# Splitting the first load of a split-GELU-multiply kernel by partitions

## The chip, the cores and the metric

The kernel runs on one core of a Trainium2 chip. The metric is the device time of one execution in microseconds. Times given are medians of several executions; besides them there is one execution taken by the hardware profiler, with its own span.

A core has compute engines that run side by side, each with its own queue of instructions. Three matter here: ScalarE (ACT in the profile), VectorE (DVE) and SyncE (SP), which only issues transfers. Transfers are carried out by 16 DMA engines, which belong to the core and serve all its queues. On-chip memory is an array of 128 partitions; a tile lies across them.

## The reference

The input `x` is 32 x 512 x 2048 float32. Its last axis is cut in two halves; the first goes through the exact GELU and is multiplied with the second:

```python
half_dim = x.shape[-1] // 2
x1, x2 = (x[..., :half_dim].copy(), x[..., half_dim:].copy())
gelu_x1 = 0.5 * x1 * (1 + erf(x1 / np.sqrt(2)))
return (gelu_x1 * x2).astype(np.float32)
```

So 134.22 MB are read and 67.11 MB written, with two operations for each element of the output.

## The kernel before

The 16,384 rows of 2048 numbers are cut into 16 tiles of 1024 rows. In a tile each of the 128 partitions holds R = 8 consecutive rows, which lie side by side in DRAM, 64 KB in one piece. There are two buffers for `x` tiles (8 MB each) and two for output tiles (4 MB each); tile i uses buffer i % 2. Tensors and semaphores are placed by hand, and the order on each engine is the order of the calls.

`load` (its transfer is issued at L47) puts a load on SP's queue. `store` (issued at L54) puts a store on a queue given to it, behind a wait for all multiplies so far. Every transfer adds 16 to a semaphore when it has landed. The page calls the queue of SP q1 and that of ACT q10.

Three loads are issued ahead of everything: rows 0 to 3 of every partition of tile 0 (32 KB in each, 4 MB in all; semaphore `first[0]`), rows 4 to 7 of tile 0 (`first[1]`), and the whole of tile 1 (`ready[1]`). Then `tc.close()` (L67) puts a barrier over the engines.

The loop over tiles comes next. In the first and the last tile the work is cut into steps of 2, 2 and 4 rows, in the others into 5 and 3 rows. In each step ACT applies GELU from the `x` tile's first half into the output tile (L81), and DVE multiplies the output tile by the `x` tile's second half in place (L89). ACT waits for the load ahead of a tile's first step; in tile 0 it waits for `first[0]` ahead of the first step and for `first[1]` ahead of the third. After a tile's last multiply SP issues the load of tile i + 2 into the same buffer. Stores are issued from ACT's queue, those of the last two tiles from SP's. A tile's load and the store of the tile two before it share a semaphore, so that ACT's one wait covers both.

At the end the semaphores are cleared (ACT at L114, DVE at L116, SP at L117), and SP waits at L118 for the last three stores.

Of the kernel before, what the change touches and what calls it, by code (L numbers as in the profile page):

```python
# [1 line left out]

# [4 lines left out]

GELU = mybir.ActivationFunctionType.Gelu


@with_exitstack
def kernel(
    ctx: ExitStack,
    tc: tile.TileContext,
    x: bass.AP,
    out: bass.AP,
):
    nc = tc.nc
    P = nc.NUM_PARTITIONS

    x_flat = x.flatten_outer_dims()
    out_flat = out.flatten_outer_dims()
    n_rows, dim = x_flat.shape
    half = dim // 2

    R = 8
    x_t = x_flat.rearrange("(n p r) d -> n p r d", p=P, r=R)
    o_t = out_flat.rearrange("(n p r) d -> n p r d", p=P, r=R)
    n_tiles = x_t.shape[0]
    x_bufs = [nc.alloc_sbuf_tensor(f"x{k}_tile", [P, R, dim], x.dtype) for k in range(2)]  # L30
    o_bufs = [nc.alloc_sbuf_tensor(f"o{k}_tile", [P, R, half], out.dtype) for k in range(2)]

    first = [nc.alloc_semaphore(f"first{j}") for j in range(2)]
    ready = [nc.alloc_semaphore(f"ready{k}") for k in range(2)]
    gelu_done = nc.alloc_semaphore("gelu_done")
    mul_done = nc.alloc_semaphore("mul_done")
    tail_stored = nc.alloc_semaphore("tail_stored")
    n = {sem.name: 0 for sem in [*first, *ready, gelu_done, mul_done, tail_stored]}  # L40

    def counted(ins, sem, by):
        ins.then_inc(sem, by)
        n[sem.name] += by

    def load(i, rows, sem):
        ins = nc.sync.dma_start(out=x_bufs[i % 2][:, rows, :], in_=x_t[i][:, rows, :])  # L47
        counted(ins, sem, 16)
        return ins

    def store(queue, i, rows, sem):
        queue.wait_ge(mul_done, n[mul_done.name])
        counted(
            queue.dma_start(out=o_t[i][:, rows, :], in_=o_bufs[i % 2][:, rows, :]), sem, 16  # L54
        )

    for ins in (  # L60
        load(0, slice(0, 4), first[0]),
        load(0, slice(4, 8), first[1]),
        load(1, slice(0, 8), ready[1]),
    ):
        tc.no_tile_sem_insts.add(ins.ins.name)
    tc.close()
    tc.compile()  # L67

    for i in range(n_tiles):
        k = i % 2  # L70
        last = i == n_tiles - 1
        pieces = i == 0 or last
        steps = ((0, 2), (2, 4), (4, 8)) if pieces else ((0, 5), (5, 8))
        for lo, hi in steps:
            rows = slice(lo, hi)
            if i == 0 and lo % 4 == 0:
                nc.scalar.wait_ge(first[lo // 4], 16)
            elif lo == 0:
                nc.scalar.wait_ge(ready[k], n[ready[k].name])
            counted(  # L80
                nc.scalar.activation(  # L81
                    out=o_bufs[k][:, rows, :], in_=x_bufs[k][:, rows, :half], func=GELU
                ),
                gelu_done,
                1,
            )
            nc.vector.wait_ge(gelu_done, n[gelu_done.name])
            counted(
                nc.vector.tensor_mul(  # L89
                    out=o_bufs[k][:, rows, :],  # L90
                    in0=o_bufs[k][:, rows, :],
                    in1=x_bufs[k][:, rows, half:],
                ),
                mul_done,
                1,
            )
            if pieces and hi % 4 == 0:
                if last:
                    store(nc.sync, i, slice(hi - 4, hi), tail_stored)
                else:  # L100
                    store(nc.scalar, i, slice(hi - 4, hi), ready[k])
        if not pieces:
            if i == n_tiles - 2:
                store(nc.sync, i, slice(0, R), tail_stored)
            else:
                store(nc.scalar, i, slice(0, R), ready[k])
        if i + 2 < n_tiles:
            nc.sync.wait_ge(mul_done, n[mul_done.name])
            load(i + 2, slice(0, R), ready[k])


    nc.scalar.drain()  # L112
    for sem in (*first, *ready):
        nc.scalar.sem_clear(sem)  # L114
    nc.vector.drain()
    nc.vector.sem_clear(gelu_done)  # L116
    nc.sync.sem_clear(mul_done)  # L117
    nc.sync.wait_ge(tail_stored, n[tail_stored.name]).then_inc(  # L118
        tail_stored, -n[tail_stored.name]
    )  # L120


# [1 line left out]
_INS = ['x']  # L124
_OUTS = [((32, 512, 1024), 'float32')]


# [23 lines left out]
```

## Time and profile before

| what | us |
|---|---|
| median of 3 runs | 469.35 |
| lowest and highest of them | 469.26 and 469.49 |
| span of the profiled execution | 467.9 |
| DVE busy in it, 34 multiplies | 140.5 |
| ACT busy in it, 34 GELUs and a table load | 115.5 |
| median from issue to landing: the two 4 MB loads of tile 0 | 16.6 |
| median from issue to landing: the 15 loads of 8 MB | 44.2 |
| median from issue to landing: the 13 stores of 4 MB from ACT's queue | 44.7 |

How to read the profile: times are counted from the start of the span. The page's second part cuts the span into 40 equal slices; each digit is the share of a slice in tenths in which an engine was busy, and the row DMA is the mean of the 16 DMA engines. The chain of waits starts at the last instruction and goes back, at each step, to what released it; printed in order of time, a row has its start, its length and what it was. In the timeline a row has the start, the length, the engine, the line, the operation, output and input, their shapes, and in brackets how long the engine stood idle before it and what ended that. The windows view gives, for a stretch A:B, its length, the busy time of each engine with the number of instructions, the granted clock of TensorE (which is not used here), the busy share of the DMA engines, and what they moved in GB/s. A share can come out a little above 1.00, since a packet's time is counted where it begins.

The trace also holds a record of each packet that the DMA engines moved: its start, its length, its size and the queue it came from, though not which of the 16 engines moved it. A packet of the first two loads has 32,768 bytes, which is what one partition gets from such a load; a packet of a load of 8 rows has 65,536 bytes. Next to them stand packets of 4 bytes, one from each engine and transfer, which count up its semaphore.

### The profile page before, as it was taken

How to read it: one execution, taken by the hardware profiler on the slowest of the kernel's cores; microseconds unless marked ns; L12 is line 12 of the kernel's file. 1: busy time of each engine (PE TensorE's matmuls, PEld its weight loads, DVE VectorE, ACT ScalarE, POOL GpSimd, SP SyncE). 2: the span in 40 equal slices, each digit the busy share in tenths (PEclk: the TensorE clock that was granted, in tenths of full speed). 3: DMA queues.
4: the chain of work that ended last, by engine and by line, in shares of the span. 5: the costliest groups of instructions: out<-in, count | busy, mean ns of one | idle time of the engine just before them, and what ended most of it. 6: DMA issues, size and time to landing. Idle time of an engine off the chain costs nothing.

```text
span 467.9 us, 152 instructions
## 1 busy us (share of the span) xinstructions
DVE 140.5 (30%) x34; ACT 115.5 (25%) x35; POOL 0.2 (0%) x4
## 2 busy tenths in 40 slices
DVE  0330514207052060511606116060150702507043
ACT  1320606042060410604106050050500506014060
POOL 0000000000000000000000000000000000000000
DMA  8999999999999999999999999999999999999998
GB/s 359 448 448 443 403 405 492 409 403 448 459 437 403 434 417 493 403 403 448 476 420 403 445 406 493 403 406 445 487 409 403 445 451 448 403 434 417 493 389 373
DMA packets 5041, 201.34 MB, mean 430 GB/s; under 512 B 560, under 2 KB 560, under 8 KB 560
## 3 DMA queue, kind: packets, MB, share of 16 engines
q1 hardware_dynamic: 2880, 142.61, 70.6%
q10 hardware_dynamic: 2160, 58.72, 29.1%
q14 instruction: 1, 0.01, 0.0%
HBM read 134.22 MB, written 67.11 MB: 430 GB/s over the span
## 4 chain that ended last, share of the span: by engine, by line
DMA 76%; DVE 14%; ACT 8%; ACTq 0%; SPq 0%; issue 0%
DMA out_dram<-o_tile 66%; DVE o_tile L89 14%; DMA x_tile<-in_x_dram 10%; ACT o_tile L81 8%; ACTq L112 0%; SPq L47 0%
## 5 line engine op out<-in xcount | busy, mean ns | idle before, releaser
L89 DVE TENSOR_TENSOR o_tile<-o_tile,x_tile 128x5120 f32<-128x5120 f32 (+3 forms) x34 | 140.5, 4171 | 319.7 <-ACT o_tile L81 319.7
L81 ACT ACTIVATE o_tile<-x_tile 128x5120 f32<-128x5120 f32 (+3 forms) x34 | 114.3, 3407 | 337.4 <-DMA out_dram<-o_tile 301.6
L81 ACT ACT_TABLE_LOAD x1 | 1.3, 1283 | 2.9 <-PEq L67 2.9
L135 POOL MEMSET const-bfloat16-1.0<- 128x1 bf16 x1 | 0.1, 101 | 0.0
L135 POOL MEMSET const-uint8-127<- 128x1 uint8 x1 | 0.1, 101 | 0.0
L135 POOL MEMSET const-float32-0.0<- 128x1 f32 x1 | 0.1, 98 | 0.2 <-issue 0.2
L135 POOL MEMSET const-float32-1.0<- 128x1 f32 x1 | 0.1, 98 | 0.0
## 6 DMA issues: line engine op xcount, KB each, us to landing
out_dram<-o_tile ACTq DMA_DIRECT2D x13, 4096.0 KB, 44.7
x_tile<-in_x_dram SPq DMA_DIRECT2D x2, 4096.0 KB, 16.6
out_dram<-o_tile ACTq DMA_DIRECT2D x2, 2048.0 KB, 34.5
out_dram<-o_tile SPq DMA_DIRECT2D x1, 4096.0 KB, 25.2
out_dram<-o_tile SPq DMA_DIRECT2D x2, 2048.0 KB, 7.8
x_tile<-in_x_dram SPq DMA_DIRECT2D x15, 44.2
```

The costliest lines, as they stand in the source:

```text
L81: nc.scalar.activation(out=o_bufs[k][:, rows, :], in_=x_bufs[k][:, rows, :half], func=GELU),
L89: nc.vector.tensor_mul(out=o_bufs[k][:, rows, :], in0=o_bufs[k][:, rows, :], in1=x_bufs[k][:, rows, half:],),
L135: nc = _bacc.Bacc("TRN2", target_bir_lowering=False, num_devices=1)
```

## The change

The first load, rows 0 to 3 of tile 0, is issued as two transfers: one for partitions 0 to 15 (512 KB, semaphore `first[0]`), and right behind it one for partitions 16 to 127 (3584 KB, a new semaphore `rest`). The loads of rows 4 to 7 and of tile 1 follow as before. Ahead of the first step of tile 0, ACT waits for both semaphores, and the new one is cleared with the others at the end. Nothing else differs; each engine's list of compute instructions is the same.

```diff
+    rest = nc.alloc_semaphore("rest")
...
-    def load(i, rows, sem):
-        ins = nc.sync.dma_start(out=x_bufs[i % 2][:, rows, :], in_=x_t[i][:, rows, :])
+    def load(i, rows, sem, parts=slice(0, P)):
+        ins = nc.sync.dma_start(
+            out=x_bufs[i % 2][parts, rows, :], in_=x_t[i][parts, rows, :]
+        )
         counted(ins, sem, 16)
         return ins
...
     for ins in (
-        load(0, slice(0, 4), first[0]),
+        load(0, slice(0, 4), first[0], slice(0, 16)),
+        load(0, slice(0, 4), rest, slice(16, P)),
         load(0, slice(4, 8), first[1]),
         load(1, slice(0, 8), ready[1]),
     ):
...
             if i == 0 and lo % 4 == 0:
                 nc.scalar.wait_ge(first[lo // 4], 16)
+                if lo == 0:
+                    nc.scalar.wait_ge(rest, 16)
...
-    for sem in (*first, *ready):
+    for sem in (*first, rest, *ready):
         nc.scalar.sem_clear(sem)
```

More of the change, by code (lines that the diff above doesn't have):

```diff
@@ L39 @@
     tail_stored = nc.alloc_semaphore("tail_stored")
-    n = {sem.name: 0 for sem in [*first, *ready, gelu_done, mul_done, tail_stored]}
+    n = {sem.name: 0 for sem in [*first, rest, *ready, gelu_done, mul_done, tail_stored]}
     def counted(ins, sem, by):
```

## The prediction

> **What bounds the kernel now.** The page comes first: its span, its shares and the row of the DMA engines.
>
> ```profile
> span 467.9 us, 152 instructions
> DVE 140.5 (30%) x34; ACT 115.5 (25%) x35; POOL 0.2 (0%) x4
> ...
> DMA  8999999999999999999999999999999999999998
> ...
> HBM read 134.22 MB, written 67.11 MB: 430 GB/s over the span
> ```
>
> No compute engine is busy for a third of the span, and the DMA digit is 9 in every slice but the first and the last. The limit is transfer. The windows view shows how complete it is.
>
> ```profile
> core 0: us, DVE busy (x) ACT busy (x) POOL busy (x), PEclk, DMA share, GB/s
> 0.00:1.70 1.70, 0.00 (x0) 0.00 (x0) 0.20 (x4) 1.00 0.00 0
> ...
> 22.00:47.00 25.00, 4.42 (x1) 3.62 (x1) 0.00 (x0) 1.00 1.02 435
> ...
> 100.00:440.00 340.00, 105.13 (x24) 85.47 (x24) 0.00 (x0) 1.00 1.00 432
> 440.00:458.00 18.00, 6.68 (x3) 7.21 (x3) 0.00 (x0) 1.00 1.00 432
> ```
>
> Nothing moves in the first 1.7 us; after that the share is 1.00 through the body. The trace's packet records sharpen this. Each of the 16 DMA engines is one unbroken row of packets, the next beginning within some 5 ns of the end of the last, from 1.74 to 2.30 us (first packets) until 466.9 to 467.4 us (last ones). All packet time divided by 16 is 466.3 us, against 465.7 us from first to last. So there is no idle time in which a delayed engine could catch up: the slowest engine's sum of packets is the time, and a microsecond lost by one engine at the start comes out at the end.
>
> Next is whether compute could leave the queues empty. The chain of waits begins so:
>
> ```profile
> 0.73 0.38 SPq L47
> 1.11 0.05 issue
> 1.16 0.42 SPq L47
> 1.59 0.05 issue
> 1.64 45.54 DMA x_tile<-in_x_dram
> 47.18 0.02 issue
> 47.20 4.48 ACT o_tile L81
> ```
>
> The loads of tiles 0 and 1 keep the engines filled to 47.2 us. The timeline shows when the next load is handed to them:
>
> ```profile
> 12.76 3.71 ACT L81 ACTIVATE o_tile<-x_tile 128x2048 f32<-128x2048 f32 x2 [8.62 <-DMA x_tile<-in_x_dram]
> ...
> 26.11 4.42 DVE L89 TENSOR_TENSOR o_tile<-o_tile,x_tile 128x4096 f32<-128x4096 f32 x1 [6.91 <-ACT o_tile L81]
> ```
>
> That multiply ends at 30.53 us and releases the load of tile 2, while tile 1 lands near 47.2: about 16.6 us of cover. ACT and DVE can be late by that much without costing anything, as long as the transfers ahead of them are late by no more.
>
> **The change, part by part.** *Issues on SP.* Two issues replace one at L47. The three issues of before start at 0.73, 1.16 and 1.64 us, so one costs about 0.45 us; the second half of tile 0 is now issued at some 1.64, tile 1 at 2.1, and the barrier behind them at L67 comes 0.45 us later. Cover: an engine's share of the first four rows lasts to about 12 us, long after any of these issues; ACT's table load (2.86 to 4.14 us) sits behind the barrier and moves to 4.6, still 8 us ahead of its data. Cost 0; without the cover 0.45 us.
>
> *Waits and clears.* ACT gets a second wait ahead of the first GELU, with all of ACT's queue behind it and DVE behind ACT. It adds nothing but the lateness of the data, since both transfers are needed as before. One more semaphore clear near 456 us (four are there, 0.07 us apart) ends long before SP's last wait at 467.85. The extra transfer brings one 4-byte packet on each engine, 9 ns and 6 ns of gap by its neighbours: +0.02 us.
>
> *The start.* First packets begin between 1.74 and 2.30 us, 1.0 us or more after the issue. If that spread is the time in which 128 rows are handed out, 16 rows take an eighth of it, and the last engine, which is also the last to end, at 467.4 us, gains up to 0.56 us. At the other end it gains nothing. I take the middle, -0.28 us. At the very most the 0.38 us of the issue would shrink away too: -0.94 us.
>
> *The first transfer, 16 neighbouring partitions.* The bytes and packets stay: one 32 KB packet per partition, 1.211 us in the steady rows (first packets 1.60 to 1.99). That is 27.06 GB/s an engine and 433 for 16, the plateau in the windows. But now all 16 engines write at the same time into 16 neighbours, an eighth of the partitions. No row of this trace does that; all data rows cover 128 partitions. Bounds: if the memory takes data by paths each as wide as one engine, at least 16 of them must lie across the 128 partitions, since 16 engines run at full rate. Sixteen neighbours then reach between 2 paths (eight neighbours to a path) and 16 (neighbours alternate). The 16 packets take 8, 4, 2 or 1 packet times: 9.69, 4.84, 2.42 or 1.21 us. The mean of the four is 4.54, the nearest case 4.84; I take that, +3.63 us on every engine, ends 0 and +8.48.
>
> [...]
>
> *The second transfer, 112 partitions.* Seven packets an engine if they are dealt out evenly. Which partition an engine takes when is not in the trace. Before, the 16 engines never collided visibly (1.211 to 1.213 us for each packet of the second round); with seven each the dealing is another one, and two engines may meet on a path, which doubles both packets. Ends for the slowest engine: none or all seven doubled, 0 to +8.48 us. I take the middle, three and a half packets, +4.24 us, because the nearest row, the clean dealing by eights, belongs to another shape and cannot vouch for this one. Nothing covers this term: the engines have no idle time.
>
> Sum: -0.28 + 0.02 + 3.63 + 4.24 = +7.6 us on the profiled span of 467.9, so 475.5. The runs have a median of 469.35, 1.5 us more than the span, for what lies around it and is untouched: **477.0 us**.
>
> [...]
>
> The lateness does not open a new wait: tile 0 lands 7.6 us later, load 2 is handed over at some 38 us, and tile 1 lands at some 55, so the 16.6 us of cover stay.
>
> **The rivals.** *Only the first transfer pays* (chance 0.22): 469.35 - 0.28 + 0.02 + 3.63 = 472.7 us. For it: the second transfer spans nearly all partitions, like every clean row. Against: seven is not eight, and the engines start on it out of the old order.
>
> *Neighbours are as good as distant partitions* (0.20), the other side: no loss, only the start's gain, 469.35 - 0.26 = 469.1 us, range 468.4 to 469.4. For it: the paths' width is unknown, and single packets run at 27 GB/s into one partition. It decides if 16 neighbours reach 16 paths.
>
> *Heavier* (0.08): two paths, +8.48, and all seven doubled, +8.48: 486.0 us.
>
> *Uneven dealing* (0.04): 112 rows by blocks of eight on 14 engines give these nine packets in place of eight, +1.21: 469.35 - 0.26 + 1.21 = 470.3 us.
>
> **How the numbers follow.** The forecast has 0.46; its own range, with the second term between one and six packets doubled, is 473.9 to 480.0. This kernel's measurement can tell about 0.2%, 0.94 us, from no change. Slower: 0.46 + 0.22 + 0.08 + 0.04 = 0.80. Of the 0.20 of no loss, 0.04 is for a start gain beyond the 0.94 worked out above as the most there could be, so faster 0.04 and same 0.16. The range runs from 469.0 to 480.0: it holds the forecast, the first and the uneven rival and most of the no-loss case, and leaves out the heavy one and gains beyond 0.35 us.
>
> **What would show it.** In the table of issues, the 512 KB transfer lands some 6.8 us after its issue (1.0 to the first packet, 0.56 of the extra that first packets have over 1.21, 4.84, and 0.35 from last data to semaphore as in the transfer of before); 3.3 us would mean the no-loss rival. The first GELU begins at 20.4 us in place of 12.76 if both terms are right, at 16.1 if only the first, at 12.5 if none. DMA digits stay 9 if a packet that waits counts as busy, while the GB/s of the first slice falls clearly. Packets of the second transfer at 2.42 us show doubling; all at 1.21 refute it. The prediction is wrong if these first packets stay below 2 us, or if the lag seen at the first GELU does not come out again, microsecond for microsecond, at the last store: then the engines had slack after all.

## The result and the profile after

The changed kernel takes 489.24 us (median of 4 runs, 488.8 to 489.78) against 469.31 for the kernel before in the same comparison: a ratio of 1.0425, 95% interval 1.0412 to 1.0438. The prediction had slower, but 477.0 us and a range that ended at 480.0. About half of the loss is what was forecast; the other half comes from a step costed at nothing.

The page of the changed kernel, first its span, busy times and the two rows in 40 slices of 12.2 us each:

```profile
span 487.5 us, 155 instructions
...
DVE 140.5 (29%) x34; ACT 115.6 (24%) x35; POOL 0.2 (0%) x4
...
DMA  8999999999999999999999999999999999999978
GB/s 177 290 440 457 448 430 393 460 433 395 454 390 446 454 387 438 436 417 430 428 425 411 452 417 414 449 398 433 425 428 433 409 444 390 436 446 409 425 328 348
```

Compute is the same to a tenth of a microsecond, and the DMA engines are as "busy" as they were. But in the first two slices they move 177 and 290 GB/s. The packets there are longer (2.8 to 4.3 us the first of each engine, up to 3.3 the next seven, against 1.21 in the steady rows of before) and count for their whole length, so the digits hide it and the bytes show it. The last two slices are low as well.

The windows of the changed kernel (stretch, its length, busy times, clock, DMA share, GB/s) tell three losses apart:

```profile
0.00:10.00 10.00, 0.00 (x0) 0.00 (x0) 0.20 (x4) 1.00 0.87 157
10.00:20.00 10.00, 0.00 (x0) 0.00 (x0) 0.00 (x0) 1.00 1.02 262
...
60.00:410.00 350.00, 105.12 (x24) 83.59 (x25) 0.00 (x0) 1.00 1.00 427
470.00:476.00 6.00, 5.00 (x3) 5.46 (x3) 0.00 (x0) 1.00 0.49 210
```

The same stretches of the kernel before; its last rows of compute come at 452 to 458 us:

```profile
0.00:10.00 10.00, 0.00 (x0) 1.28 (x1) 0.20 (x4) 1.00 0.91 367
10.00:20.00 10.00, 4.49 (x2) 3.71 (x2) 0.00 (x0) 1.00 0.97 419
...
60.00:410.00 350.00, 105.59 (x25) 85.47 (x24) 0.00 (x0) 1.00 1.00 433
452.00:458.00 6.00, 5.19 (x3) 3.78 (x2) 0.00 (x0) 1.00 0.98 423
```

A slow start was expected. Not expected were a body at 427 GB/s in place of 433, at full share, and engines that stand idle half of the time just before the last stores. The idle time ends with the first store of the last tile. In the changed kernel it is issued at 474.70 us, and every engine that had stopped takes packets again from 475.6; in the kernel before, it is issued at 455.03 us, while the store of tile 14 still runs (it lands at 458.1). First the row of the changed kernel, then that of the kernel before:

```profile
474.70 0.34 SPq L57 DMA_DIRECT2D out_dram<-o_tile  x1
```

```profile
455.03 0.34 SPq L54 DMA_DIRECT2D out_dram<-o_tile  x1
```

The timeline of the changed kernel around its first compute holds the clue. A row's bracket is the engine's idle time before it and what ended it.

```profile
23.08 1.28 ACT L87 ACT_TABLE_LOAD   x1 [23.08 <-DMA x_tile<-in_x_dram]
24.37 3.71 ACT L87 ACTIVATE o_tile<-x_tile 128x2048 f32<-128x2048 f32 x2
...
30.84 0.38 ACTq L57 DMA_DIRECT2D out_dram<-o_tile  x1
```

The data of the first half tile are there at 23.0 us, 10.3 later than before (12.74). But ACT's table load, which ran at 2.86 us before, now starts only with the data. The view of L83, the line of the second wait (the one for `rest`), shows why:

```profile
L83 ACTq EVENT_SEMAPHORE  x1: 17/17/17, 23.0 to 23.0; - x1
```

The second wait stands on ACT's queue as an instruction of its own, and the table load comes behind it. The first wait, for `first[0]`, has no instruction of its own; the trace's record has it on the GELU itself, as in the kernel before. Had the wait for `first[0]` been the one ahead of the table load, the load could have run from 7.8 us, when the 512 KB had landed, and been over by an estimated 9.2. The two waits in the other order were not run. So the first store is issued at 30.84 us, 11.6 us later than before, where the data account for 10.3.

### The profile page after: what moved, and what is told of

Same layout as the page of the kernel before. It is cut to its first block, busy times and chain, and to the rows that moved or that the text cites. A ratio compares the mean times of both kernels' runs of the same rounds, so it can differ in the third digit from the quotient of the medians.

```text
span 487.5 us, 155 instructions
## 1 busy us (share of the span) xinstructions
DVE 140.5 (29%) x34; ACT 115.6 (24%) x35; POOL 0.2 (0%) x4
## 4 chain that ended last, share of the span: by engine, by line
DMA 72%; DVE 14%; ACT 8%; another core or an unknown queue 3%; ACTq 0%; SPq 0%; issue 0%
DMA out_dram<-o_tile 65%; DVE o_tile L95 14%; ACT o_tile L87 8%; DMA x_tile<-in_x_dram 6%; ACTq L118 0%; SPq L48 0%; ACTq L57 0%
```

## The experiments

Each has the kernel before beside it in the same runs (469.28 to 469.36 us). Spans of the profiled executions are compared with the 467.9 us of before. Edits that remove or move the changed kernel's split load are shown against the changed kernel, the others against the kernel before; lines that only declare or clear a semaphore are left out.

### Is the late table load the other half?

**One semaphore and one wait for both parts of the split load, without `rest`:**

```diff
-        load(0, slice(0, 4), rest, slice(16, P)),
+        load(0, slice(0, 4), first[0], slice(16, P)),
...
-                nc.scalar.wait_ge(first[lo // 4], 16)
-                if lo == 0:
-                    nc.scalar.wait_ge(rest, 16)
+                nc.scalar.wait_ge(first[lo // 4], 32 if lo == 0 else 16)
```

> Both parts of the split load count on one semaphore and ACT has one wait for 32, as it had one wait before; the transfers stay as in the changed kernel. In its profile the first half of tile 0 lands at 23.0 us, about 10 us late, but the span grew by 19.6: the other 9 us are lost later, in slower first packets of each tile's load and in a ragged end. Theory A: the second wait pushed ACT's table load (1.28 us) behind the data, the first store came too late to join tile 1's load at its first packet, and stores trail loads by a packet from then on; then this kernel gets the table load back ahead of the data and loses only the 10 us: about 479.5. Theory B: the 16 engines leave the start out of step (by up to 1.3 us), and that costs the later 9 us; then the time stays near 489.

478.54 us (478.37 to 481.36), ratio 1.021 (1.0182 to 1.0239). Its timeline and windows:

```profile
3.32 1.28 ACT L84 ACT_TABLE_LOAD   x1 [3.32 <-PEq L70]
...
29.43 0.38 ACTq L56 DMA_DIRECT2D out_dram<-o_tile  x1
```

```profile
0.00:10.00 10.00, 0.00 (x0) 1.28 (x1) 0.20 (x4) 1.00 0.90 157
10.00:20.00 10.00, 0.00 (x0) 0.00 (x0) 0.00 (x0) 1.00 1.01 262
60.00:410.00 350.00, 110.56 (x26) 89.39 (x26) 0.00 (x0) 1.00 1.00 435
460.00:466.00 6.00, 5.19 (x3) 5.27 (x2) 0.00 (x0) 1.00 0.99 426
```

The start is as slow as in the changed kernel, to the GB/s; the body and the end are clean. Span 477.2 us: 9.3 us of the 19.6 belong to the split transfers, 10.3 to the table load behind the wait. The engines leave the start as much out of step as in the changed kernel (their last packets of tile 0 end up to 1.1 us apart; 1.3 there), so theory B falls.

**Both waits kept, the table loaded early** by a GELU on one column of a free tile, added to the changed kernel:

```diff
+    nc.vector.memset(o_bufs[1][:, 0:1, 0:1], 0.0).then_inc(warm, 1)
+    nc.scalar.wait_ge(warm, 1)
+    nc.scalar.activation(
+        out=o_bufs[1][:, 0:1, 0:1], in_=o_bufs[1][:, 0:1, 0:1], func=GELU
+    )
     for i in range(n_tiles):
```

> The changed kernel with both its semaphores and waits, and a GELU on one column of the free output tile ahead of the waits, so that the table is loaded early. Theory A: the first store is issued at about 29.5 us and only the start's 10 us remain, 478.5. If the two waits themselves delay or the steps after them matter, it stays near 489.

478.34 us, ratio 1.0192 (1.0177 to 1.0207). So it is the place of the table load, not the number of waits or semaphores.

**A second wait alone, added to the kernel before, no transfer changed:**

```diff
                 nc.scalar.wait_ge(first[lo // 4], 16)
+                if lo == 0:
+                    nc.scalar.wait_ge(first[0], 16)
```

> The kernel before, with nothing changed but a second wait of ACT on the same semaphore and count ahead of the first GELU. No transfer differs. The table load should hang on the extra wait and start with the data, at about 12.8 us, and the first store be issued 1.4 us later, at 20.6. If the late table load is the whole cause of the later loss (theory A), this costs what the row split cost, 473 to 477 us, with some of the 16 engines taking the first store's packets one load packet later than others. If it needs the split as well, 469.3.

469.30 us in the middle of 10 runs, but three of them took 471.05, 472.83 and 473.50; ratio 1.0019 (0.9997 to 1.0041). In the profiled execution, a clean one, the table load starts at 12.84 us and the first store is issued at 20.60, and every engine still takes that store's packets in the order of before. This delay lands on an edge: mostly it costs nothing. The expectation of a steady 473 to 477 missed.

**The split by rows, all partitions in each part, with the changed kernel's two waits:**

```diff
-        load(0, slice(0, 4), first[0], slice(0, 16)),
-        load(0, slice(0, 4), rest, slice(16, P)),
+        load(0, slice(0, 2), first[0]),
+        load(0, slice(2, 4), rest),
```

> The first load is cut in two by rows (0 and 1, then 2 and 3), each over all 128 partitions, with the changed kernel's two semaphores and two waits. If the loss comes from the partitions that a transfer covers, nothing is lost at the start: first half landed at about 12.8 us and, unless the late table load costs something by itself, 469.4. If theory A holds for the later loss by the table load alone, up to 9 us more, 478. If merely having two transfers costs the 10 us, 479 or more.

475.17 us (473.26 to 476.75), ratio 1.0125 (1.0091 to 1.0159). Nothing is lost at the start: the data are there at 12.8 us. With the store issued at 20.62 us, four of the 16 engines missed its old place, twelve did not. Most of the 5.5 us by which its span is longer (473.4) is idle time near the end, 3.8 us an engine on average. The row split with one wait was not run.

### What the late store does

The packet records show which place that is. Counted is how many packets of tile 1's load (65,536 bytes, 2.42 us each) an engine runs before its first store packet, and the mean length of such packets from 60 to 410 us:

| kernel | first store issued, us | load packets before the first store packet | mean load packet, ns |
|---|---|---|---|
| before | 19.23 | 1 on all 16 engines | 2418 |
| one wait | 29.43 | 1 on all | 2418 |
| row split | 20.62 | 1 on twelve, 2 on four | 2426 |
| changed | 30.84 | 2 on fifteen, 1 on one | 2482 |

Behind this, loads and stores alternate on every engine. With one packet before, the store of a tile and the load issued together with it finish together on an engine (their last packets 0.01 us apart in the kernel before); with two, the store's last packet, the one of 4 bytes that counts up the semaphore, comes behind the first packet of the next load, for the rest of the run (from 110 to 436 us of the changed kernel 3.4 us after the load's). Nine tenths of the slow packets in the changed kernel are the second or third of a tile's load, mostly 0.1 to 0.6 us longer (0.4 in the middle). To see whether the lag itself costs, and which lag, it was set in the kernel before, with no split.

**First store behind the third GELU in ACT's queue:**

```diff
+            if i == 0 and lo == 4:
+                store(nc.scalar, 0, slice(0, 4), ready[0])
             nc.vector.wait_ge(gelu_done, n[gelu_done.name])
...
+            if i == 0 and hi == 4:
+                continue
             if pieces and hi % 4 == 0:
```

> The kernel before with the first store issued after the third GELU in ACT's queue, some 3 to 7 us later, so that every one of the 16 engines must miss the place that it took, none just so. If stores that trail the loads by a packet or two cost time by themselves, this loses as much as or more than the row split: 475 to 480. If it is the mixture, some engines in the one order and some in the other, that costs, all engines keep one order here and nothing is lost: 469.3.

477.70 us, ratio 1.0178 (1.0163 to 1.0194). Issued at 22.63 us, the store comes behind two load packets on all 16 engines, and the body and the end look as in the changed kernel (mean load packet 2474 ns):

```profile
60.00:410.00 350.00, 101.80 (x24) 85.47 (x24) 0.00 (x0) 1.00 1.00 427
461.00:466.00 5.00, 4.19 (x3) 4.51 (x2) 0.00 (x0) 1.00 0.60 259
```

So a store 3.4 us late loses 8.4 us without any split, and without a mixture of orders among the engines; the mixture is not needed.

**The same, and the store also waits for the end of the third GELU:**

```diff
             if i == 0 and lo == 4:
+                nc.scalar.wait_ge(gelu_done, n[gelu_done.name])
                 store(nc.scalar, 0, slice(0, 4), ready[0])
```

> As the kernel with the late first store (issued at 22.6 us, stores one load packet late, 477.7 us), but the store also waits for the end of the third GELU, some 3.5 us more, so that it should come a further load packet late on every engine, still in two pieces. The kernel that stored tile 0 whole, four or five packets late, lost only 0.9 us. If a lag of one packet is what collides, this is close to that one, 469.5 to 471. If it is the two pieces and any lag, 477 to 479.

472.33 us, ratio 1.0062 (1.0046 to 1.0079), between the two expectations. Issued at 26.13 us, the store comes behind four load packets on all engines, not the three expected. The body is clean and the end still idles, 2.2 us an engine:

```profile
60.00:410.00 350.00, 103.62 (x24) 85.47 (x24) 0.00 (x0) 1.00 1.00 435
456.00:461.00 5.00, 4.19 (x3) 3.89 (x2) 0.00 (x0) 1.00 0.49 210
```

**Tile 0 stored in one piece at 30.6 us:**

```diff
+            if i == 0:
+                if hi == R:
+                    store(nc.scalar, i, slice(0, R), ready[k])
-            if pieces and hi % 4 == 0:
+            elif pieces and hi % 4 == 0:
```

> The kernel before with tile 0 stored in one piece at 30.6 us in place of two pieces at 19.2 and 30.6, so that its stores come about four load packets later than before, where the late first store of the earlier run came one later (477.7 us). If what costs is that a load and its partner store no longer end together on an engine, it costs again about 8 us per whole run, 477 or more. If only a lag of just one packet collides, 469.3. If stores late by much leave the loads ahead and the end covered, as little as 469.

470.20 us (ten runs, 469.79 to 471.42), ratio 1.0024 (1.0014 to 1.0034), near neither 469.3 nor 477. Five or six load packets come first, the mean load packet is 2418 ns again, and the end has no gap. A later store is thus cheaper than a store one packet late. The slow body belongs to the lag of one packet, in the lags tried; a lag of two packets was not met.

### What the split transfers cost

Here an extra transfer stands ahead of a whole first load and fills the second output tile, which is free until tile 1. Its bytes are work added. ACT waits for it ahead of tile 1's first step.

```diff
...
+        ins = nc.sync.dma_start(out=o_bufs[1][0:16, :, :], in_=x_t[0][0:16, 0:4, :].rearrange("p a (c e) -> p (a c) e", e=half))
...
     for ins in (
+        load_extra(),
         load(0, slice(0, 4), first[0]),
```

The others differ in the partitions alone: `0:128:8`, `16:128`, and all.

> The kernel before with one extra transfer ahead of all: 32 KB into each of partitions 0 to 15 of the second output tile, which is free then. The first load is whole again. It moves one packet more on each engine (+1.2 us). If the first of the two terms is what I measured in the changed kernel (packets of 2.8 to 4.3 us, mean 3.6, against 1.8 for a first packet), it costs 1.2 + 1.9 to 2.5, so 472.5 to 473.0, and the 112-partition transfer made the rest. If first packets out of step are enough to cost the later 9 us, 481.

> As the kernel with an extra transfer of 16 partitions (473.4 us, first packets 2.8 to 4.3 us), but to partitions 0, 8, 16 and so on to 120. [...] If 16 partitions are slow for being few, it is 473.4 again.

> The kernel before with an extra transfer of the second half of the split alone, 32 KB into each of partitions 16 to 127 of the free output tile, ahead of a whole first load. Its bytes cost 7 packets an engine, 8.5 us: 477.8. In the changed kernel these packets took about 2.2 us in place of 1.21. If that is how 112 partitions are dealt out, it happens here too: 7 times 1.0 more, 484.5 to 485.5. If it came from starting out of step behind the 16-partition transfer, 477.8 to 478.5.

> The control for the extra transfers: the same over all 128 partitions. Its bytes cost 8 packets an engine, 9.7 us, and everything behind is late by as much. If lateness and an extra transfer cost nothing of themselves, 479.0; anything above is a cost that the other extra transfers would share.

The four results, with the bytes taken at 1.22 us for each packet of an engine, as the transfer over all 128 partitions has it (9.8 us of span for 8). A packet's length is the mean over the engines; the base for a first one is 1.74 us, for later ones 1.21.

| partitions of the extra transfer | time, us | ratio | span less 467.9 | less its bytes | its packets, us |
|---|---|---|---|---|---|
| 0 to 15 | 473.40 | 1.0087 (1.0072 to 1.0102) | 4.0 | 2.8 | 3.8 |
| 0, 8, ... 120 | 471.73 | 1.0051 (1.0034 to 1.0068) | 2.1 | 0.9 | 2.4 |
| 16 to 127 | 482.83 | 1.0288 (1.0273 to 1.0304) | 13.6 | 5.1 | 1.5 to 2.2 |
| 0 to 127 | 479.05 | 1.0207 (1.0192 to 1.0222) | 9.8 | - | 1.7, then 1.21 |

The control adds its bytes and no more, so lateness and an extra transfer cost nothing by themselves. By the medians of the runs the spread partitions lose 1.2 us in place of 0.9; the other losses stay within 0.1. Sixteen neighbours thus cost two to three times what sixteen spread partitions cost, so it is their neighbourhood more than their number. And 112 partitions are slow without the other part ahead of them, though less than expected: 482.83 us lies between the 484.5 to 485.5 of equally slow packets and the 477.8 to 478.5 of clean ones.

Neighbouring partitions are also neighbours in DRAM here, 64 KB apart, in each of these runs and in the next. The runs don't tell apart whether the on-chip end or the DRAM end of such a transfer holds it back.

**The cut at partition 64:**

```diff
-        load(0, slice(0, 4), first[0], slice(0, 16)),
-        load(0, slice(0, 4), rest, slice(16, P)),
+        load(0, slice(0, 4), first[0], slice(0, 64)),
+        load(0, slice(0, 4), rest, slice(64, P)),
```

> The cut is at partition 64 in place of 16; all else as in the changed kernel. If neighbouring partitions share paths of one engine's width, of which 64 neighbours reach half, each half takes twice its time: packets of 2.4 us throughout, first half landed at some 22 us, some 479 to 489 us. If what counts is that 16 neighbours are few, or that 112 does not deal out in eights, 64 and 64 deal out evenly by fours and lose nothing: 469.5.

489.37 us (486.08 to 490.42), ratio 1.0415 (1.0377 to 1.0453). In its windows the rate is half of the plateau through the first 20 us, at full share:

```profile
0.00:10.00 10.00, 0.00 (x0) 0.00 (x0) 0.20 (x4) 1.00 0.96 203
10.00:20.00 10.00, 0.00 (x0) 0.00 (x0) 0.00 (x0) 1.00 1.01 210
```

Packets settle at 2.56 us where all partitions give 1.21. Here the dealing is even, four packets an engine in each half, and still everything behind the first packets doubles: 64 neighbours take data at half the rate of 128 (210 GB/s from 10 to 20 us, against 419 in the kernel before). The late store follows as in the changed kernel (two load packets first on 15 engines).

## Why the prediction was wrong

- **What bounds the kernel** was right. The engines had no slack: extra bytes came out again in full (9.8 us of span for 8 packets), and the start's loss stayed to the end nearly whole (in the kernel with one wait 10.2 us at the first GELU, 9.3 in the span).
- **Waits and clears** is the step that failed. It said that the second wait "adds nothing but the lateness of the data", and the paragraph on issues had the table load move only to 4.6 us, "still 8 us ahead of its data". The second wait stood ahead of the table load; that put 1.28 us between the data and the first GELU and made the first store some 1.4 us late. The cost is 10.3 us of span (487.5 against 477.2 with one wait). Of these, 6.9 are longer packets (all packet time divided by 16 is 482.1 us against 475.2). In the changed kernel an engine also idles 2.8 us on average near the end, with one wait none; the remaining 0.6 us is in part the engines' uneven ends. The prediction weighed cover only by whether "compute could leave the queues empty", and found 16.6 us by which ACT and DVE could be late "without costing anything". That cover held: tile 2's load was issued at 40.84 us, 16 us ahead of tile 1's landing. But a store 3.4 us late costs 8.4 us in the kernel before. The prediction did not ask where in the queues the store would fall; there the table load's 1.4 us were enough.
- **The first transfer** was put at 3.63 us by four shared paths, an assumption of the author's; alone it cost 2.8. That neighbours are slower than spread partitions is what the runs show (2.8 us lost against 0.9); no run shows such paths, and none excludes the DRAM end of the transfers.
- **The second transfer** was put at 4.24; alone it cost 5.1. Its packets are nearly all lengthened, to means of 1.5 to 2.2 us by their place in the row, not some doubled and some clean. Both parts together cost 9.3, 1.4 more than the sum of the two alone.
- **The start** gained nothing: first packets begin between 1.75 and 2.50 us, against 1.74 to 2.30. Fewer rows in the first transfer did not start the last engine sooner.
- With the table load left early, the forecast of 477.0 stands against 478.3 and 478.5. That is near by some luck: the first term was 0.8 us too high and the second 0.9 too low, the start's gain did not come, and the 1.4 us that the two parts cost together were in no term.
- **Of the rivals**, none held the second half. "No loss" and "only the first transfer pays" fall by the extra transfers. The heavy one came near the size (486.0) by doublings that did not happen, and uneven dealing is excluded by the packets: in the run with the 112-partition transfer alone every engine moves seven of them ahead of its first 4-byte packet.
- **The signs named ahead**: first GELU at 20.4 us expected, data at 23.0 and GELU at 24.37 found; landing of the 512 KB after 6.8 expected, 7.1 found, but not by the same parts: the packets took 4.3 us at most, not 5.4, and from the last data to the semaphore it took 1.4 us, not 0.35. The first packets stayed above the 2 us below which the prediction would have been wrong (2.8 to 4.3); those of the second transfer kept neither to 1.21 nor to 2.42 us (1.5 to 3.3). The test "microsecond for microsecond" pointed the right way: 11.6 us of lag at the first GELU became 19.6 at the end, which no start could explain.

What stays open: why a lag of one packet lengthens the second and third load packets of each tile, when lags of three packets or more do not; why the end idles with lags of one and three packets and not with four or five; in which order 112 partitions are dealt to the engines; and at which end of a transfer neighbours cost.

## What to carry to other kernels

When a wait is added ahead of an engine's first use of a function table, look in the trace for where the wait went: here one of two waits became an instruction ahead of the table load and held it back behind the data, from 2.86 us to 23.08. In a kernel bound by transfers, a delay that no engine seems to need can still change the order in which loads and stores share the DMA engines, and here that order lasted to the end of the run (a store issued 3.4 us late cost 8.4); test it by moving the issue alone. Don't cut a transfer by partitions to have its first part sooner: cut by rows, which lost nothing at the start here (data at 12.8 us, against 23.0 with the cut at partition 16), and keep all 128 partitions in each part.

## What had not been expected of the hardware

- A store issued 3.4 us late, a move of 0.7% of the run, costs 8.4 us; 6.9 us late it costs 3.0; and as one piece, 11.4 us late, 0.9. The cost is not monotonic in the delay.
- From its issue to its first packet this store took at least 5.14 us in the kernel before and 3.73 in the changed kernel, though engines had ended a load packet sooner. In the changed kernel the one engine whose load packet ended 3.73 us after the issue took up the store at once; the fifteen whose packet ended 2.4 to 3.4 us after the issue ran another load packet first. In the kernel whose store waits for the third GELU, load packets that ended 2.7 to 3.2 us after the issue were too early on all 16 engines.
- 64 of 128 partitions, evenly dealt to all 16 engines, take 2.56 us a packet in place of 1.21: with half of the partitions, which are neighbours, a little less than half of the rate.
